# DeltaNet chunks of 128 tokens, an inverse joined from blocks of 32 and 64, and projections given out in two pieces

## The chip, the cores and the metric

The kernel runs on one core of a Trainium2 chip. The metric is device time in microseconds (us) of the whole program: one layer of a hybrid decoder on 1024 tokens of width 1024, in float32. Engines are named as in the profile: PE is TensorE's products and PEld its weight loads, DVE is VectorE, ACT ScalarE, POOL GpSimd, and SP the SyncE queue that issues the DMAs.

## The reference

The layer normalizes x, projects it, runs two token mixers beside each other (a gated DeltaNet and a sparse attention, NSA), merges both by gates, and ends with an MLP. The change touches the DeltaNet alone. Its core, cut to what matters:

```python
DN_HEADS, DN_HEAD_DIM, DN_CHUNK = 8, 128, 64
qkv = silu(causal_depthwise_conv(qkv, conv_w))            # 4 taps
q, k = l2norm(q), l2norm(k);  beta = sigmoid(b_logit)
g = -exp(a_log) * softplus(a_logit + dt_bias)
# per head and chunk of C tokens
gc = cumsum(g);  kb = k * beta;  vb = v * beta
decay = exp(where(causal, gc_i - gc_j, -inf))
a = where(strict, (kb @ k.T) * decay, 0)
u = triangular_solve(a + eye(C), vb)
w = triangular_solve(a + eye(C), kb * exp(gc))
qk = (q @ k.T) * decay;  q_dec = q * exp(gc);  k_end = k * exp(gc_last - gc)
# scan over the chunks, state S (128 x 128)
v_new = u - w @ S
o = q_dec @ S + qk @ v_new
S = S * exp(gc_last) + k_end.T @ v_new
# output: rmsnorm(o) * out_norm * silu(z)
```

The result does not depend on the chunk's length but for rounding: a longer chunk makes fewer steps of the scan and a larger triangular matrix to invert.

## The kernel before, in words

Everything is laid out with features or tokens on the 128 partitions. A projection of the normalized x is a unit of 128 output columns: its weights are read in two DMAs, split on ScalarE and VectorE into a high and a low part (`wh`, `wl`, so that float32 accuracy comes from three fast products), and multiplied with two halves of 512 tokens. One half is 24 products of 128x512, written to a PSUM bank `g` (two banks in turn). A unit of `fill_nb` (the NSA's keys, values and queries) is computed the other way around, in 8 tiles of 128 tokens with 24 products of 128x256 each.

The program is written by a table of due times. `at(step, rank, fn)` enters a function; at the end all are sorted by step and rank and called, and the framework's scheduler then places each engine's instructions. One step is about one half of a projection, 24 streamed products. A head (`head(h, s0)`) covers 24 steps and a new one starts every 14, so the work of two heads overlaps: steps s0 to s0+7 project k, q, v and the gate z with their convolutions; s0+8 to s0+13 are filled with one unit of `fill_nb` and one of `fill_rows` (merge gates); the inverse stands at s0+11 to s0+14, `u_w` at s0+15, and the 16 chunks of 64 tokens from s0+16, three a step, beside the next head's projections.

For a half of 512 tokens (four tiles of 128, two chunks each) `k_natural` and `k_turn` normalize k and make `kbe`, `ke` and the decay matrices `dm`, `qk`; `k_k` and `k_q` multiply k with k and with q. These, the inverse and `u` work on 64 by 64 quadrants of TensorE, the two chunks of a tile on partitions 0 to 63 and 64 to 127. The inverse starts in `blocks`: the diagonal 16 by 16 blocks of all 64 places of a head go through DRAM (`asc`) into a tile of 64 partitions, VectorE eliminates in 15 steps of two small instructions (`xt`, `xi`), and the result comes back through DRAM (`xzs`) as `xa` and its transpose `za`. Then `inv_y` and `inv_x` join blocks of 16 to 32 (level 0) and 32 to 64 (level 1), with a product, an eviction, a product and a subtraction each. `u_w` makes u and w. A `chunk` is a chain: a product with the state (`c<-St,wq`), VectorE's subtraction (`vn`), two products (`c<-vn,ke`, `c<-vn,qk`), VectorE's new state (`St`), and ScalarE's eviction of the output (`o`). Large elementwise products (`kbe`, `ke`, the masks `n1` and `n2`, beta into `dm`, the norm of `o`) run on GpSimd.

After the eighth head come the sparse attention, the merge and the MLP; neither is touched.

Of the kernel before, what the change touches and what calls it, by code (L numbers as in the profile page):

```python
# [30 lines left out]
CH = 64  # L31
# [3 lines left out]
CONST = (("ident", "tri", "blk", "ones", "anyv"), ("m1", "m2", "l1", "l2"),  # L35
# [7 lines left out]
def constants():  # L43
# [4 lines left out]
    same = (p // CH) == (c // CH)  # L48
    ident = (p == c).astype(f)
    tri = (same & (p <= c)).astype(f)  # L50
    blk = same.astype(f)
    i, j = p % CH, np.arange(CH)[None, :]
    m1 = np.where(j < i, 0, 1e30).astype(f)
    m2 = np.where(i <= j, 0, -1e30).astype(f)
    l1 = ((i // 32 == j // 32) & (i // 16 != j // 16)).astype(f)
    l2 = (i // 32 != j // 32).astype(f) + 0 * m1
# [40 lines left out]
    parts = dict(ident=ident, tri=tri, blk=blk, ones=np.ones((128, 128), f), m1=m1, m2=m2, l1=l1, l2=l2, msel=msel,  # L97
# [49 lines left out]
def body(ctx: ExitStack, tc: tile.TileContext, A, out):  # L147
# [146 lines left out]
    def proj(ps, ks, half):  # L294
        sl = slice(half * 512, (half + 1) * 512)
        gemm(ps, [(ks[k][0], ks[k][1], hh[:, k, sl], hl[:, k, sl]) for k in range(8)])
# [100 lines left out]
    def gating():  # L397
# [41 lines left out]
        mm(pg, K("blk"), ln.rearrange("p h t -> p (h t)"), True, True)  # L439
# [143 lines left out]
    def bm(n):  # L583
        return K(n).unsqueeze(1).to_broadcast([128, 4, 64])
# [11 lines left out]
    Q2 = [slice(0, 64), slice(64, 128)]  # L596


    vns = []

    qks = [pd.tile([128, 6, 64], F32, name=f"qk{i}", bufs=1) for i in range(3)]
    for a in qks:
        GP.memset(a, 0.0)
    turn_q = [0]
# [21 lines left out]
    def pairs(l, r):  # L626

        p = PL.ps.tile([128, 4, 64], F32, name="s")
        for i in range(4):
            for q in Q2:  # L630
                mm(p[q, i, :], l[:, i, q], r[:, i, q], True, True)
        return p

# [7 lines left out]

    def move(ap, sl, t, load):

        for q in Q2:
            d = dense(ap, sl)[q, :, q]
            SY.dma_start(t[q] if load else d, d if load else t[q])

    def head(h, s0):
# [11 lines left out]
        def conv(s, half):  # L660

            c0 = 20 + (s * 8 + h) * 4
            ps = gtile()
            proj(ps, H["w", s], half)
# [30 lines left out]
        def k_turn(half):  # L695
# [12 lines left out]
            ut = t4("dm", 2, 64)  # L708
            for q in Q2:
                V.tensor_tensor(ut[q], H["gcB"].rearrange("p (t c) -> p t c", c=128)[q, sl, q],  # L710
                                b3(gc[:, h, sl], 64)[q], OP.subtract)
            H["qk", half] = qks[turn_q[0] % 3]
            turn_q[0] += 1
            dt = H["qk", half][:, 1:5]
# [4 lines left out]
            GP.tensor_tensor(ut, ut, b3(beta[:, h, sl], 64), OP.mult)  # L719
# [12 lines left out]
        def blocks():  # L732
# [17 lines left out]
            for half in range(2):  # L750
                H["x", half], H["z", half] = d = t4("xa", 2, 64), t4("za", 2, 64)
                for j in range(2):
                    move(xz[j], S4[half], d[j], True)

        def row_decay():
            gcB = H["gcB"]
            H["gl"] = gl = pd.tile([128, 16], F32, name="gl", bufs=2)
            act(gl, gcB[:, CH - 1::CH], AF.Exp)
            act(gcB, gcB, AF.Exp)

        def q_sums(half):

# [3 lines left out]
            for i in range(4):  # L766
                for q, o in (Q2, Q2[::-1]):
                    mm(ps[o, i:i + 1], sq[:, i, q], K("ones")[:, 0:1], True, True)
# [5 lines left out]
        def k_q(half):  # L774
            ac = H.pop(("ac", 0, half))
            dt = H["qk", half][:, 1:5]
            V.tensor_tensor(dt, dt, pairs(H["kT", half], ac), OP.mult)
            w = pd.tile([128, 4, 256], F32, name="wq", bufs=2)
            GP.tensor_tensor(w[:, :, 64:192], ac, H["gcB"].rearrange("p (t c) -> p t c", c=128)[:, S4[half]],
                             OP.mult)  # L780
            H["wq", half] = w
# [6 lines left out]

        def gate(half):
            ps = gtile()  # L790
            proj(ps, H["w", 3], half)
# [7 lines left out]
        def inv_y(level, half):  # L799
            H["y", half] = y = t4("y", 2, 64)  # L800
            act(y, each(H["n", half][level], H["z", half]))

        def inv_x(level, half):
            x, z, y = H["x", half], H["z", half], H["y", half]
            p = each(x, y)
            if level == 0:
                p2 = each(y, x)
                V.tensor_tensor(z, z, p, OP.subtract)
                V.tensor_tensor(x, x, p2, OP.subtract)
            else:  # L810
                for q in Q2:
                    V.tensor_tensor(zs[half][q, :, q], z[q], p[q], OP.subtract)

        def u_w(half):
            z, vb = zs[half], H["vb", half]
            u = t2("u", 2)
            p = PL.ps.tile([128, 4, 128], F32, name="s")
            for i in range(4):
                for q in Q2:
                    mm(p[q, i, :], z[q, i, q], vb[q, i, :], True, True)  # L820
            act(u, p)
            H["u", half] = u
            p = four(H["kbe", half], z)
            w = H["wq", half]
            act(w[:, :, 0:64], p[:, :, 0:64])
            act(w[:, :, 192:256], p[:, :, 64:128])

        def chunk(c):
            half, i, q = c // 8, (c % 8) // 2, c % 2
            P_ = slice(64 * q, 64 * q + 64)  # L830
            Q_ = slice(64 - 64 * q, 128 - 64 * q)
            if c % 8 == 0:
                H["o", half] = t2("o", 2)
            o, u, St = H["o", half], H["u", half], H.get("S")
            vn = vns[q]
            ps = PL.pc.tile([128, 128], F32, name="c")
            if St is None:
                V.tensor_copy(vn[P_], u[P_, i, :])
            else:
                mm(ps, H["wq", half][:, i, q * 128:(q + 1) * 128], St, True, False)  # L840
                V.tensor_tensor(vn[P_], u[P_, i, :], ps[P_], OP.subtract)
            if c < 15:
# [7 lines left out]

            k = 64 * (i + q)
            mm(ps, H["qk", half].rearrange("p a b -> p (a b)")[:, k:k + 128], vn, St is None, True)
            act(o[Q_, i, :], ps[Q_], AF.Copy, scale=H["rq", half][Q_, i:i + 1])

        def out_norm(half):
# [6 lines left out]
            GP.tensor_tensor(o, o, b3(ss), OP.mult)  # L862

        def out_turn(half):
            pt = flip(H["o", half], "pc", "c")
            of = t2("of", 1)
            for q in range(2):
                a, b = slice(64 * q, 64 * q + 64), slice(64 - 64 * q, 128 - 64 * q)
                V.scalar_tensor_tensor(of[:, :, a], pt[:, :, b], og, H["sz", half][:, :, a],
                                       op0=OP.mult, op1=OP.mult)  # L870
# [3 lines left out]
        for i, s in enumerate((1, 0, 2, 3)):  # L874
            at(s0 + 2 * i - 2, 2, prep, s)
            for half in range(2):
                if s < 3:
                    at(s0 + 2 * i + half, 1, conv, s, half)
                else:
                    at(s0 + 2 * i + half, 1, gate, half)  # L880
        for half in range(2):
# [6 lines left out]
            at(s0 + 11, 0, inv_y, 0, half)  # L888
# [870 lines left out]
```

## Time and profile before

| what | value |
| --- | --- |
| timed runs, median (lowest to highest) | 2386.36 us (2383.36 to 2388.78) |
| the profiled execution | 2383.02 us, span 2381.2 us |
| busy: PE, PEld | 2330.4 us, 1911.3 us |
| busy: DVE, ACT, POOL | 1600.7 us, 1100.0 us, 292.6 us |
| granted TensorE clock over the span | 0.997 of full |
| one DeltaNet head, first inverse product to the next head's | 112.2 us |

Busy time of PE counts each product to a modelled end, and products overlap, so two of them that start 0.23 us apart are shown with 0.39 us each; the distance of starts is what one costs. A float32 product leaves two records, a transpose one. The streamed products run on a split type and leave one. Idle time is put down to what released the engine; on an engine that is not waited for it costs nothing.

### The profile page before, as it was taken

What the parts mean: (1) busy time and instruction counts of PE and PEld (TensorE: products, weight loads), DVE (VectorE), ACT (ScalarE), POOL (GpSimd) and SP (SyncE); (2) the same over time, 40 slices, a digit from 0 to 9 for tenths busy, and PEclk for the clock granted to TensorE, in tenths of its full rate; (3) what the DMA queues carried; (4) which work ended last, traced back from release to release, by engine and by line L of the source; (5) the groups of instructions that cost most, each with busy time, mean ns of one, the idle gap of its engine ahead of it and who ended that gap; (6) DMA issues with size and microseconds to landing.
All of it is one profiled execution on the core that took longest, in us unless ns stands there. A gap on an engine that the chain in (4) does not pass through costs nothing.

```text
span 2381.2 us, 44200 instructions
## 1 busy us (share of the span) xinstructions
PE 2330.4 (98%) x16657; PEld 1911.3 (80%) x16657; DVE 1600.7 (67%) x3846; ACT 1100.0 (46%) x2274; POOL 292.6 (12%) x299
## 2 busy tenths in 40 slices
PE   7999999999999999999999999999999999999999
PEld 5887878787878797877777778778877888888887
DVE  7666665747574847347868686745498777786875
ACT  4233333424343443226766666542356555544443
POOL 1132321202232333000011111000000000000000
PEclk9999999999999999999999999999999999999999
DMA  6421313131312122227532332055424443495333
GB/s 196 119 62 60 86 43 91 42 94 35 92 46 79 51 70 59 83 83 205 142 110 82 111 94 69 24 179 181 169 102 177 151 155 124 175 325 190 120 115 102
DMA packets 237382, 267.37 MB, mean 112 GB/s; under 512 B 76848, under 2 KB 128368, under 8 KB 237040
## 3 DMA queue, kind: packets, MB, share of 16 engines
q1 hardware_dynamic: 237168, 264.55, 35.3%
q8 instruction: 131, 2.15, 0.4%
q14 instruction: 83, 0.68, 0.1%
HBM read 190.05 MB, written 72.38 MB: 110 GB/s over the span
## 4 chain that ended last, share of the span: by engine, by line
PE 49%; DVE 2%; DMA 1%; ACT 0%; issue 0%; POOL 0%; SPq 0%; ACTq 0%; POOLq 0%; DVEq 0%
PE V L177 20%; PE Q L177 12%; PE T L177 5%; PE o L177 5%; PE g L177 3%; PE S L177 2%; PE m L177 1%; PE m L1280 0%; DVE big L1482 0%; DMA o<-ond 0%; DVE junk L1226 0%; PE m L1193 0%; DMA a<-gtd 0%; POOL acc L1275 0%; DMA ra<-odd 0%
## 5 line engine op out<-in xcount | busy, mean ns | idle before, releaser
L177 PE MATMUL g<-hh,wh 128*128 128x512 f32 (+1 forms) x816 | 336.7, 413 | 7.1 <-ACT hh L174 6.3
L177 PE MATMUL g<-hl,wh 128*128 128x512 f32 (+1 forms) x816 | 328.5, 403 | 0.4 <-DVE hl L327 0.3
L177 PE MATMUL g<-hh,wl 128*128 128x512 f32 (+1 forms) x816 | 325.0, 398 | 0.1
L174 ACT ACTIVATE wh<-a 128x512 fp32r<-128x512 f32 x234 | 146.6, 629 | 248.7 <-PE V L177 155.0
L177 PE MATMUL V<-big,wh 128*128 128x512 f32 x768 | 236.8, 390 | 0.8 <-DVE c L1601 0.8
L1226 DVE CUSTOM_DVE_ANT_0 junk<-S,cst 128x384 f32<-128x384 f32 (+3 forms) x320 | 168.3, 532 | 56.1 <-PE S L177 52.1
L177 PEld LDWEIGHTS g<-hh,wh 128*128 128x128 f32 (+1 forms) x816 | 154.3, 189 | 35.8 <-ACT hh L174 6.8
L174 ACT ACTIVATE P<-T 128x512 f32<-128x512 f32 x228 | 134.2, 597 | 103.4 <-PE T L177 90.5
L186 DVE TENSOR_TENSOR wl<-a,wh 128x512 fp32r<-128x512 f32 x192 | 131.6, 687 | 74.5 <-ACT wh L174 74.4
L177 PEld LDWEIGHTS g<-hh,wl 128*128 128x128 f32 (+1 forms) x816 | 154.2, 189 | 29.3 <-DVE wl L277 0.5
L177 PEld LDWEIGHTS g<-hl,wh 128*128 128x128 f32 (+1 forms) x816 | 154.4, 189 | 28.4 <-DVE hl L327 3.4
L174 ACT ACTIVATE wh<-wr 128x512 fp32r<-128x512 f32 x168 | 105.7, 629 | 153.5 <-PE g L177 127.7
L177 PEld LDWEIGHTS V<-big,wh 128*128 128x128 f32 x768 | 144.1, 188 | 31.5 <-DVE c L1601 1.2
L277 DVE TENSOR_TENSOR wl<-wr,wh 128x512 fp32r<-128x512 f32 x136 | 94.7, 701 | 90.5 <-ACT wh L174 89.5
L177 PE MATMUL V<-big,wl 128*128 128x512 f32 x384 | 149.5, 389 | 0.9 <-DVE wl L277 0.9
L177 PE MATMUL g<-wh,hh 128*128 128x256 f32 x512 | 147.3, 288 | 0.0
L177 PE MATMUL g<-wl,hh 128*128 128x256 f32 x512 | 144.8, 283 | 0.0
L177 PE MATMUL g<-wh,hl 128*128 128x256 f32 x512 | 144.8, 283 | 0.0
L177 PEld LDWEIGHTS o<-vv,P 128*64 128x64 f32 x3648 | 116.0, 138 | 27.1 <-issue 20.4
L177 PE MATMUL o<-vv,P 128*64 128x65 f32 x3648 | 130.1, 225 | 0.0
L177 PE MATMUL S<-ks,qc 96*128 96x384 f32 (+3 forms) x320 | 125.9, 405 | 2.0 <-DVE mx L1226 1.6
L676 DVE SCALAR_TENSOR_TENSOR acc<-xp,cols,acc 128x512 f32<-128x512 f32 x144 | 117.1, 813 | 6.3 <-ACT acc L174 4.8
(381 smaller groups left out, 5462.0 us busy)
## 6 DMA issues: line engine op xcount, KB each, us to landing
bb<-acd SPq DMA_DIRECT2D x112, 256.0 KB, 2.7
wr<-in_w_dn_dram SPq DMA_DIRECT2D x64, 256.0 KB, 2.8
a<-in_w_u_dram SPq DMA_DIRECT2D x64, 256.0 KB, 2.6
acd<-c SPq DMA_DIRECT2D x64, 256.0 KB, 2.2
a<-in_w_d_dram SPq DMA_DIRECT2D x64, 256.0 KB, 3.4
wr<-in_w_nb_dram SPq DMA_DIRECT2D x32, 256.0 KB, 2.7
wr<-in_w_gt_dram SPq DMA_DIRECT2D x32, 256.0 KB, 2.6
gtd<-fx SPq DMA_DIRECT2D x32, 256.0 KB, 2.1
```

Source lines behind the costliest of these rows:

```text
L174: return SC.activation(o, i, fn, **kw)
L177: return PE.matmul(o, l, r, start=start, stop=stop, skip_group_check=True)
L186: V.tensor_tensor(lo, src, f(hi), OP.subtract)
L277: V.tensor_tensor(wl, wr, f(wh), OP.subtract)
L676: V.scalar_tensor_tensor(a2, xp[:, i:i + 512], cols[:, c0 + i:c0 + i + 1], a2, op0=OP.mult, op1=OP.add)
L1226: V.tensor_tensor_reduce(junk[:, :w], ps[:, :w], mask[:, a:b], 1.0, 3e38, OP.add, OP.min, o)
```

## The change

The constant `CH` becomes 128: a tile of 128 tokens is one chunk, so the state goes through 8 steps a head. The decay matrices, masks and products of k with k and with q cover 128 by 128 and use all of TensorE's array. The triangular matrix to invert is 128 wide: one masked level (16 to 32) stays on 64 by 64 quadrants, `join_y` and `join_x` make 64 of 32 with products of 32 columns, and `last_y` and `last_x` make 128 of 64. What GpSimd multiplied is done by four ScalarE instructions each (`rows_by`), or folded into VectorE's instruction on PSUM (`k_k`). A projection's half is given out as `first` (12 products) and, half a step later, the other 12, and `blocks` stands 1.5 steps later. The diff, cut to its core:

```diff
-CH = 64
+CH = 128
...
-    def proj(ps, ks, half):
+    def proj(ps, ks, half, part=(0, 8)):
...
+    def rows_by(o, i, col):
+
+        for j in range(4):
+            act(o[:, j], i[:, j], AF.Copy, scale=col[:, j:j + 1])
...
-            GP.tensor_tensor(kb, kn, b3(beg[:, h, sl]), OP.mult)
+            rows_by(kb, kn, beg[:, h, sl])
...
-            GP.tensor_tensor(k2, kn, b3(ek[:, h, sl]), OP.mult)
+            rows_by(k2, kn, ek[:, h, sl])
...
-            V.tensor_tensor(dm, dm, pairs(H["kT", half], H["kT", half]), OP.mult)
-            move(a_, S4[half], dm, False)
-            n1 = t4("n1", 2, 64)
-            GP.tensor_tensor(n1, dm, bm("l1"), OP.mult)
-            n2 = t4("n2", 2, 64)
-            GP.tensor_tensor(n2, dm, bm("l2"), OP.mult)
-            H["n", half] = (n1, n2)
+            p = four(H["kT", half], H["kT", half])
+            for j in range(4):
+                t = 4 * half + j
+                V.scalar_tensor_tensor(dm[:, j], p[:, j], beta[:, h, t:t + 1], dm[:, j], op0=OP.mult, op1=OP.mult)
+            H["n", half] = n1 = t4("n1", 2, 64)
...
+        def first(s, half):
+            H["g"] = gtile()
+            proj(H["g"], H["w", s], half, (0, 4))
...
+        def join_y(half):
+            dm, z = H["dm", half], zs[half]
+            H["y", half] = y = t4("y", 2, 64)
+            p = PL.ps.tile([128, 4, 64], F32, name="s")
+            for i in range(4):
+                for o in (0, 64):
+                    mm(p[o:o + 32, i, 0:32], dm[o:o + 64, i, o:o + 32], z[o:o + 64, i, o + 32:o + 64], True, True)
+            for o in (0, 64):
+                act(y[o:o + 32, :, 0:32], p[o:o + 32, :, 0:32])
+
+        def join_x(half):
+            x, y, z = H["x", half], H["y", half], zs[half]
+            p = PL.ps.tile([128, 4, 64], F32, name="s")
+            for i in range(4):
+                for o in (0, 64):
+                    mm(p[o:o + 32, i, 0:32], x[o:o + 32, i, 0:32], y[o:o + 32, i, 0:32], True, True)
+                mm(p[32:64, i, 0:32], y[0:32, i, 0:32], x[0:32, i, 0:32], True, True)
+            for o in (0, 64):
+                act(z[o:o + 32, :, o + 32:o + 64], p[o:o + 32, :, 0:32], AF.Copy, scale=-1.0)
+            act(x[32:64, :, 0:32], p[32:64, :, 0:32], AF.Copy, scale=-1.0)
+
+        def last_y(half):
+            a, b = Q2
+            H["y", half] = y = t4("y", 2, 64)
+            p = PL.ps.tile([128, 4, 64], F32, name="s")
+            for i in range(4):
+                mm(p[a, i, :], H["dm", half][b, i, a], zs[half][b, i, b], True, True)
+            act(y[a], p[a])
...
+            act(u, four(zs[half], H["vb", half]))
             H["u", half] = u
...
+            act(H["wq", half][:, :, 0], four(H["kbe", half], zs[half]))
...
+                mm(ps[:, 0], wq[:, i, 0], St, True, True)
+                mm(ps[:, 1], wq[:, i, 1], St, True, False)
+                vn = PL.p2.tile([128, 128], F32, name="vn", bufs=2)
+                V.tensor_tensor(vn, u[:, i], ps[:, 0], OP.subtract)
+            if c < 7:
...
-            at(s0 + 11, 0, inv_y, 0, half)
...
+            at(s0 + 10.5, 0, inv_y, half)
...
-        at(s0 + 5, 0, blocks)
-        for c in range(16):
-            at(s0 + 16 + c // 3, -2, chunk, c)
+        at(s0 + 6.5, 0, blocks)
+        for c in range(8):
+            at(s0 + 16 + c / 2, -2, chunk, c)
```

`last_x` does with `x` and `y` what `last_y` does, and writes the corner of `zs` with the sign turned.

The order of the instructions moves with it. TensorE, a middle head's chunks beside the next head's first projection, before (`St` is the state, `g` a projection's bank, the numbers tell buffers apart):

```order
L177 MATMUL c<-vn_1118,ke 128x128
L177 MATMUL c<-vn_1118,qk_426 128x128
L177 MATMUL g<-hl,wh 128x512
L177 MATMUL g<-hh,wl 128x512
L177 MATMUL c<-St,wq 128x128
L177 MATMUL g<-hh,wh 128x512
L177 MATMUL g<-hl,wh 128x512
L177 MATMUL g<-hh,wl 128x512
L177 MATMUL c<-vn_1116,ke 128x128
```

and the same place after the change:

```order
L174 MATMUL c<-St,wq 128x128 x2
L174 MATMUL g<-hh,wh 128x512
L174 MATMUL g<-hl,wh 128x512
L174 MATMUL g<-hh,wl 128x512
L174 MATMUL g<-hh,wh 128x512
L174 MATMUL g<-hl,wh 128x512
L174 MATMUL g<-hh,wl 128x512
L174 MATMUL c<-vn,ke 128x128
L174 MATMUL c<-vn,qk 128x128
```

Between two links of the chain stand six streamed products where two or three stood, and a link has two products with the state.

TensorE, the second half of a middle head's inverse, before (`za`, `xa` are the inverse and its transpose, `n` the masked matrix, `vb` the values):

```order
L177 MATMUL s<-za,n_4748 64x64 x8
L177 MATMUL s<-za,n_4894 64x64 x8
...
L177 MATMUL s<-y,xa 64x64 x16
...
L177 MATMUL s<-vb,zs_422 64x128 x8
L177 MATMUL s<-zs_422,kbe 128x128 x4
```

and after (`zs` is the joined inverse):

```order
L174 MATMUL s<-zs_422,dm 32x32 x8
L174 MATMUL s<-zs_423,dm 32x32 x8
...
L174 MATMUL s<-y,xa 32x32 x2
L174 MATMUL s<-xa,y 32x32
...
L174 MATMUL s<-zs_422,dm 64x64 x4
L174 MATMUL s<-zs_423,dm 64x64 x4
...
L174 MATMUL s<-y,xa 64x64 x8
...
L174 MATMUL s<-vb,zs_422 128x128 x4
L174 MATMUL s<-zs_422,kbe 128x128 x4
```

One join of two groups has become two joins of two groups each; the pairs of 32 columns stand eight times in a row, for two halves.

VectorE, the start of a middle head's block inverse, before (`ab` is the loaded matrix, `xi` the inverse, `acc` the convolution of v, `vn` and `St` the last chunks of the head ahead):

```order
L744 TENSOR_TENSOR xt<-ab,xi 64x15
L849 SCALAR_TENSOR_TENSOR St<-St,gl,c 128x128
L746 TENSOR_TENSOR xi<-xi,xt 64x15
L676 SCALAR_TENSOR_TENSOR acc<-xp,cols,acc 128x512
L744 TENSOR_TENSOR xt<-ab,xi 64x28
L841 TENSOR_TENSOR vn_1118<-u,c 64x128
L746 TENSOR_TENSOR xi<-xi,xt 64x14x2
```

and after:

```order
L724 TENSOR_TENSOR xt<-ab,xi 64x15
L659 SCALAR_TENSOR_TENSOR acc<-xp,cols,acc 128x512
L726 TENSOR_TENSOR xi<-xi,xt 64x15
L867 TENSOR_REDUCE oss<-of 128x4
L724 TENSOR_TENSOR xt<-ab,xi 64x28
L663 SCALAR_TENSOR_TENSOR acc<-xp,acc 128x512
L726 TENSOR_TENSOR xi<-xi,xt 64x14x2
```

The rows of the chunks are gone from it; the block inverse now begins when the last chunk is done.

## Rows read from the trace of the kernel before

**Rows 1.** The page: span, and each engine's busy us, share, instructions.

```profile
span 2381.2 us, 44200 instructions
PE 2330.4 (98%) x16657; PEld 1911.3 (80%) x16657; DVE 1600.7 (67%) x3846; ACT 1100.0 (46%) x2274; POOL 292.6 (12%) x299
```

**Rows 2.** Stretch of one head: length, busy us by engine (instructions), clock, DMA.

```profile
core 0: us, PE busy (x) PEld busy (x) DVE busy (x) ACT busy (x) POOL busy (x), PEclk, DMA share, GB/s
396.96:509.16 112.20, 109.45 (x861) 92.48 (x860) 66.74 (x160) 39.97 (x78) 22.62 (x20) 1.00 0.23 66
```

**Rows 3.** Timeline of PE, steady projection: start, us, instruction.

```profile
521.18 0.39 PE L177 MATMUL g<-hh,wl 128*128 128x512 f32 x1
...
523.67 0.39 PE L177 MATMUL g<-hl,wh 128*128 128x512 f32 x1
```

**Rows 4.** Timeline of PE at an inverse product among token products.

```profile
508.83 0.28 PE L177 MATMUL g<-wl,hh 128*128 128x256 f32 x1
508.95 0.28 PE L177 MATMUL g<-wh,hl 128*128 128x256 f32 x1
509.16 1.15 PE L177 MATMUL s<-za,n 64*64 64x64 f32 x32
510.24 0.39 PE L177 MATMUL g<-wh,hh 128*128 128x256 f32 x1
510.46 0.28 PE L177 MATMUL g<-wl,hh 128*128 128x256 f32 x1
```

**Rows 5.** Timeline of PE: `u` of a half, then pairs, sums, transposes, chunk.

```profile
537.71 1.09 PE L177 MATMUL s<-vb,zs 64*64 64x128 f32 x16
538.74 1.16 PE L177 MATMUL s<-zs,kbe 128*128 128x128 f32 x8
...
565.24 0.69 PE L177 MATMUL s<-kT 128*64 128x64 f32 x16
565.76 0.58 PE L177 MATMUL tp<-cst,tmp 128*64 128x1 f32 x16
566.27 0.44 PE L609 MATMUL tp<-cst,nat 128*128 128x128 f32 x2
566.55 0.39 PE L177 MATMUL c<-vn,ke 128*128 128x128 f32 x2
566.77 0.39 PE L177 MATMUL c<-vn,qk 128*128 128x128 f32 x2
567.00 0.38 PE L609 MATMUL tp<-cst,nat 128*128 128x128 f32 x2
```

**Rows 6.** Waits of PE, 100 to 1080 us: us in total, times, longest.

```profile
PE c L177 <- DVE vn L841: 8.6, 20, 0.6
PE c L177 <- DVE xi L746: 3.2, 6, 1.2
```

**Rows 7.** Timeline of PE: the last chunk's wait, and one in the chain.

```profile
487.16 0.49 PE L177 MATMUL c<-vn,qk 128*128 128x128 f32 x2 [0.59 <-DVE vn L841]
...
569.99 0.49 PE L177 MATMUL c<-St,wq 128*128 128x128 f32 x2
...
571.59 0.46 PE L177 MATMUL c<-vn,ke 128*128 128x128 f32 x2 [0.41 <-DVE vn L841]
```

**Rows 8.** Timeline of DVE and POOL where both are busy.

```profile
456.59 0.75 DVE L676 SCALAR_TENSOR_TENSOR acc<-xp,cols,acc 128x512 f32<-128x512 f32 x1
457.64 1.39 DVE L676 SCALAR_TENSOR_TENSOR acc<-xp,cols,acc 128x512 f32<-128x512 f32 x1
458.44 1.49 POOL L706 TENSOR_TENSOR ke<-nat,ek 128x512 f32<-128x512 f32 x1
```

**Rows 9.** ScalarE's group of output evictions, 100 to 1080: busy us, mean ns.

```profile
L174 ACT ACTIVATE o<-c,rq 64x128 f32<-64x128 f32 x128 | 46.3, 362 | 130.9 <-PE c L177 120.4 <-DVE acc L676 7.7 <-DVE xp L667 1.9
```

**Rows 10.** Timeline of DVE and SP: one head's block inverse and its DMAs.

```profile
477.51 0.17 DVE L744 TENSOR_TENSOR xt<-ab,xi 64x15 f32<-64x15 f32 x1 [1.63 <-DMA ab<-asc]
493.96 0.37 DVE L747 COPY xi<-xi 64x256 f32<-64x256 f32 x1
493.46 1.47 SPq L749 DMA_DIRECT2D xzs<-xi  x2
496.21 1.26 SPq L646 DMA_DIRECT2D xa<-xzs  x2
500.16 1.27 SPq L646 DMA_DIRECT2D za<-xzs  x2
```

More of the change, by code (lines that the diff above doesn't have):

```diff
@@ L624, in each @@
         return p
[L626 to L632, printed above, removed]
     def diag(ap):
@@ L752, in blocks @@
                 for j in range(2):
-                    move(xz[j], S4[half], d[j], True)
+                    for q in Q2:
+                        SY.dma_start(d[j][q], dense(xz[j], S4[half])[q, :, q])
         def row_decay():
             gcB = H["gcB"]
-            H["gl"] = gl = pd.tile([128, 16], F32, name="gl", bufs=2)
+            H["gl"] = gl = pd.tile([128, 8], F32, name="gl", bufs=2)
             act(gl, gcB[:, CH - 1::CH], AF.Exp)
@@ L766, in q_sums @@
             for i in range(4):
[L767 to L768 removed]
+                mm(ps[:, i:i + 1], sq[:, i, :], K("ones")[:, 0:1], True, True)
             rq = pd.tile([128, 4], F32, name="rq", bufs=4)
@@ L775, in k_q @@
             ac = H.pop(("ac", 0, half))
[L776 to L779, printed above, removed]
+            dt = H["qk", half]
+            V.tensor_tensor(dt, dt, four(H["kT", half], ac), OP.mult)
+            w = pd.tile([128, 4, 2, 128], F32, name="wq", bufs=2)
+            GP.tensor_tensor(w[:, :, 1], ac, H["gcB"].rearrange("p (t c) -> p t c", c=128)[:, S4[half]],
                              OP.mult)
@@ L797, in gate, with inv_y, inv_x @@
             H["sz", half] = s_
-        def inv_y(level, half):
+        def inv_y(half):
             H["y", half] = y = t4("y", 2, 64)
-            act(y, each(H["n", half][level], H["z", half]))
-        def inv_x(level, half):
+            act(y, each(H["n", half], H["z", half]))
+        def inv_x(half):
             x, z, y = H["x", half], H["z", half], H["y", half]
             p = each(x, y)
[L806 to L812, printed above, removed]
+            p2 = each(y, x)
+            for q in Q2:
+                V.tensor_tensor(zs[half][q, :, q], z[q], p[q], OP.subtract)
+            V.tensor_tensor(x, x, p2, OP.subtract)
@@ new lines, in last_y, with last_x @@
+        def last_y(half):
[5 more added lines that the diff above has]
+            act(y[a], p[a])
+        def last_x(half):
+            a, b = Q2
+            p = PL.ps.tile([128, 4, 64], F32, name="s")
+            for i in range(4):
+                mm(p[a, i, :], H["x", half][a, i, :], H["y", half][a, i, :], True, True)
+            act(zs[half][a, :, b], p[a], AF.Copy, scale=-1.0)
@@ L866, in out_turn @@
             of = t2("of", 1)
[L867 to L870, printed above, removed]
+            V.scalar_tensor_tensor(of, pt, og, H["sz", half], op0=OP.mult, op1=OP.mult)
             SY.dma_start(odd[h, :, half * 512:(half + 1) * 512], flat(of))
@@ L876, in head @@
             for half in range(2):
+                at(s0 + 2 * i + half, 1, first, s, half)
                 if s < 3:
-                    at(s0 + 2 * i + half, 1, conv, s, half)
+                    at(s0 + 2 * i + half + 0.5, 1, conv, s, half)
                 else:
-                    at(s0 + 2 * i + half, 1, gate, half)
+                    at(s0 + 2 * i + half + 0.5, 1, gate, half)
         for half in range(2):
@@ L915, in go, with plan @@
             SY.dma_start(dst[:, half * 512:(half + 1) * 512], x)
-        return prep, [lambda s, i=i: at(s, 1, go, i) for i in range(2)]
+        def plan(s, half):
+            at(s, 1, begin, half)
+            at(s + 0.5, 1, go, half)
+        return prep, [lambda s, i=i: plan(s, i) for i in range(2)]
     def fill_nb(u):
@@ L991, in tail_b @@
         pool("p2", side="right")
-        for i in range(2):
-            vns.append(PL.p2.tile([128, 128], F32, name=f"vn{i}", bufs=1))
-            GP.memset(vns[i], 0.0)
     def tail_c():
```

114 lines of the change are left out of this document (47 added, 67 removed).

## The prediction

> **What bounds the kernel now.** I read the page's busy shares first: TensorE is busy for 98% of the span, VectorE for 67%, ScalarE for 46%, GpSimd for 12% [rows 1]. The profiled run took 2383.0 us, 1.8 us more than its span, and 3.4 us less than the median of the three timed runs, 2386.4; I work against 2383.0 and add the 3.4 at the end. Next the stretches: one period of the DeltaNet stage, from one head's first inverse product to the next head's, is 112.2 us at full granted clock, with TensorE marked busy for 109.45 [rows 2]. Eight such periods are the only place where the change acts. So time comes or goes only as TensorE's work in a period, or its waits there, come or go. "Busy" hides part of the waits, because ends of pipelined products are modelled; so I count from one start to the next instead.
>
> **A ledger of one period.** A streamed product of a projection takes 0.2264 us (11 steps from 521.18 to 523.67) [rows 3]; one of the 256-wide token products takes 0.12 us (508.83 to 508.95) [rows 4]. A full float32 product of 128 columns leaves two records of 0.1125 us (four in 0.45 us, 566.55 to 567.00), so 0.225 us; 64-column quadrant products take 0.034 us a record (32 in 1.08 us), 64-column ones over 128 rows 0.0325 (16 in 0.52), one-column sums 0.032 (16 in 0.51), 64-row ones of 128 columns 0.064 (16 in 1.03) [rows 4, 5]. Going from streamed products to small ones and back costs more: 508.95 to 510.46 is 1.51 us, of which one streamed product is 0.12 before, the records 1.08 and one 0.12 after, so about 0.19 us for a round trip [rows 4].
>
> From the code, a period has 240 streamed (54.3 us), 192 token products (23.0), 46 chunk products (15 `St,wq`, 15 `ke`, 16 `qk`: 10.4), 32 transposes (one record each, 3.6), 8 products for `kbe` (1.8), and small ones: 160 records of inverse (5.4), 64 of key and query pairs (2.1), 32 of query sums (1.0), 32 for `u` (2.0), together 10.5. That is 103.6. With 12 round trips, 2.3, it is 105.9, and 6.3 us of the 112.2 are left: waits. The waits I can see belong to the chunk chain. VectorE's `vn` released TensorE 20 times and the rows of the block inverse (`xi`, ahead of `vn` on VectorE) six times [rows 6]; an example is `c<-St,wq` at 569.99, three streamed products, then 0.41 us idle before `c<-vn,ke` at 571.59; the last chunk waits 0.59 us at 487.16 [rows 7].
>
> **The change, part by part, per head.**
>
> *Chunks of 128.* Eight steps instead of sixteen. Seven have two `St,wq` (14), seven a `ke`, eight a `qk`: 29 products against 46. Minus 17 times 0.225 is **-3.8 us**, and this term has no bounds worth the name.
>
> *Pairs, sums and `u` without quadrants.* Key and query pairs become 16 full products, 32 records of 0.1125, 3.6 instead of 2.1. `u` becomes 8 full ones, 1.8 instead of 2.0. The one-column sums become 16 records over 128 stationary columns; the trace has 0.032 for 64 stationary columns and 0.1125 for 128, so 0.5 to 1.8; I take 1.6, near the row with the same stationary size.
>
> *The inverse.* One masked level of 64 by 64 stays: 96 records at 0.034, 3.3. The two last products are 32 records in a single quadrant, where neighbours cannot overlap: between 0.034 (two quadrants in turn) and half of the full 0.1125; I take the upper, 1.8, since that is what 64 columns cost alone. The joins of 32-blocks are 40 products, 80 records of 32 columns, which no row shows. From below the one-column row, 0.032, 2.6; from above half a full record, 4.5; I take 0.034, the nearest small shape, 2.7. The Trainium skill (TensorEngine Tiling (Array Packing), Instruction Overhead) says that a product of few columns costs as much as one of some 60 cycles; by it, an estimate, 25 ns a record, the joins would be 2.0 and the sum 6 us lower over eight heads. No row here goes as low, so I keep the row.
>
> Small work after: 3.6 + 1.8 + 1.6 + 3.3 + 1.8 + 2.7 = 14.8 against 10.5, **+4.3 us** (bounds +2.5 and +6.5). Round trips: pairs, sums and `u` no longer need one; the seven groups of the inverse do, so 7 against 12: **-1.0 us** (0 to -1.5).
>
> *Waits.* In the order of before, three or four streamed products (0.7 to 0.9 us) stand between `c<-St,wq` and `c<-vn,ke`, and two between `ke` and the next `St,wq`; in the new order six and six (1.36 us) at most places. The link needs VectorE's subtraction plus its turn in a queue whose entries take up to 0.75 us, or 1.39 us beside GpSimd [rows 8]. So 1.36 us covers most links; three of seven have fewer products to cover them, and the last head has three streamed ones. The block inverse also moves 1.5 steps later, behind the last chunk, so `xi` no longer stands ahead of `vn`. I give 2.0 us to the seven links and 0.5 us to the handovers of the joins: 2.5 instead of 6.3, **-3.8 us** (bounds 0 and -5.3).
>
> *What costs nothing.* GpSimd's products of `kbe`, `ke` and the output go to ScalarE, four instructions each. At 0.362 us, the row of `o<-c,rq` that has this width [rows 9], 24 more of them a head are 8.7 us, on an engine with 40 us busy in 112 [rows 2]; that leaves ScalarE under half, and `kbe` and `ke` are read only a dozen steps later, by `u_w` and the chunks. What the bursts may delay instead is in rival 2. Masks of 512 columns instead of 256 on VectorE are balanced by half as many `St` and `vn`. Giving a projection out in two pieces moves no product; it only lets a chunk stand every half step. A constant table is 128 columns shorter at the start: under half a microsecond.
>
> *A wait that could grow.* The block inverse is a chain by way of DRAM: its first VectorE row starts at 477.51 and its copy at 493.96, 16.4 us, of which about 30 tiny rows are 6 us and the rest other work; two stores follow at 493.46, eight loads until 501.43, and the first inverse product waits until 509.16, so some 5 us of slack after a landing of about 2 us, the time from first store to first load being 2.75 [rows 4, 10]. Moved 1.5 steps later (8.2 us), with the product half a step earlier (2.9 us), the slack would be -6 us; but nine `St` and `vn` and the masks of the next head leave its VectorE stretch, by the order about 4 us of work, and its load is issued at the head of the gate step instead of a projection's tail (2.5 us). I make it near +1 us: no wait, but no cover.
>
> *Sum.* -3.8 + 4.3 - 1.0 - 3.8 = -4.3 us a head. The first head fills and the last drains differently (three streamed products only); I take 7.5 heads, -32 us: 2351 for the profiled run, **2354 us** against the median, 1.3% faster.
>
> **Rivals.**
> 1. *The waits stay.* If VectorE and ScalarE answer as late as now, the chain keeps its 6.3 us: -0.5 us a head, 2382, about no change. For it: the last chunk waited though nine streamed products stood before it [rows 7], so distance alone does not cure a late queue. Against it: that VectorE stretch held the block inverse, which moves. 13%.
> 2. *The inverse becomes the wait (slower).* Place: the first inverse product of each head, and the five handovers PE, ScalarE, PE behind it at one half-step (2.7 us) each. If the block inverse takes as long as now after its first row, its loads land 3 to 4 us after the product's turn, and five handovers at 0.7 us, one row of ScalarE queue, add 3.5: 7 us a head, 8 heads, +56 on 2354, 2410. It decides from 4.3 us of new waits a head. A burst of eight ScalarE rows (2.9 us) ahead of an `o` that frees the chunk's bank would act in the same way. Against it: VectorE and ScalarE are idle for 45 and 72 us of the 112 [rows 2]. 11%.
> 3. *More comes back.* With GpSimd's large products gone, VectorE's 1.39 us instruction beside `ke` (1.49 us on GpSimd) is 0.75 us again, and no chunk waits: 2.5 us a head more, and cheap joins, 1 us: 7.5 times 3.5 is 26 more, 2328. The Trainium skill (SBUF — State Buffer, "SBUF: two separate sides") says that GpSimd and a VectorE instruction with two SBUF inputs exclude each other for a whole instruction; the 1.39 beside 0.75 [rows 8] agrees, and by the rule this rival gains most. Against it: VectorE is not the bound, so what it gains reaches the end only where TensorE waited. 14%.
>
> **How the numbers follow.** My forecast, -32 give or take 16 us (2338 to 2372), has 62%. Its terms at their favourable bounds give -8 us a head, 2322; at the unfavourable ones +2.7, 2407. From these and the rivals the range for 8 in 10 is 2328 to 2384. About 0.2%, 5 us, is what a measurement of this kernel can tell from no change: the forecast, rival 3 and a quarter of rival 1 make faster 0.81; the rest of rival 1 and a little of rival 2 make the same 0.10; slower 0.09.
>
> **What would show it.** Right: a period near 108 us; `St,wq`, `ke` and `qk` records near 29 products a head at 0.11 us; joins near 0.03 us a record; no idle row over 0.3 us before `c<-vn,ke` in the middle heads; GpSimd busy under 200 us. Wrong: joins near 0.06 us, idle time before `s<-za,n` released by a load of `xa` or `za`, or before `s<-zs,dm` and `s<-vb,zs` released by ScalarE; or a period still near 112 us, with the waits on `vn` as long as now.

## The result, and the profile after

The changed kernel took 2354.89 us, median of four runs (2353.76 to 2355.44), against 2385.77 us of the kernel before in the same session: a ratio of 0.9869, 95% interval [0.9852, 0.9886], or 27 to 35 us less. The forecast was 2354. The number came out; the step on the waits behind it did not, nor did all that was put at nothing, and two parts of the change turned out to work against each other.

The page of the profiled execution, in answer to [rows 1]; it took 2355.1 us:

```profile
span 2353.3 us, 43197 instructions
PE 2306.0 (98%) x16257; PEld 1917.6 (81%) x16257; DVE 1567.3 (67%) x3742; ACT 1155.6 (49%) x2482; POOL 184.2 (8%) x198
```

TensorE is busy for 24 us less, GpSimd for 108 us less, ScalarE for 56 us more. One head, in answer to [rows 2] (length, busy time by engine, granted clock):

```profile
495.96:606.07 110.11, 107.10 (x816) 93.63 (x815) 65.44 (x158) 48.75 (x110) 12.91 (x12) 1.00 0.24 67
```

From first inverse product to first inverse product, the first six periods were 113.0 us on average before (170.79 to 848.60) and are 109.9 now (166.96 to 826.55): 3.0 us a head, where 4.3 were forecast. These six periods whole, before and after (length, busy time of TensorE and of the others):

```profile
170.79:848.60 677.81, 664.44 (x5225) 561.99 (x5224) 428.07 (x1056) 261.58 (x533) 170.50 (x152) 1.00 0.23 66
```

```profile
166.96:826.55 659.59, 645.53 (x4925) 565.51 (x4924) 401.91 (x979) 303.01 (x689) 89.91 (x80) 1.00 0.24 67
```

TensorE's idle time, length less busy time, was 13.4 us and is 14.1 us: 2.2 and 2.3 us a head. The gain is all in its products. Giving each of TensorE's rows the time up to the next row's start, less the idle time that the timeline shows between them, splits a head's period so (us, mean of the six, each figure rounded for itself):

| | before | after | difference |
| --- | --- | --- | --- |
| the chunks' products | 10.1 | 6.2 | -3.9 |
| small work: pairs, sums, `u`, inverse | 11.0 | 14.1 | +3.1 |
| transposes and the products for `kbe` | 6.5 | 6.1 | -0.3 |
| streamed and token products, the same 432 | 83.2 | 81.2 | -2.0 |
| idle | 2.2 | 2.3 | +0.1 |
| period | 113.0 | 109.9 | -3.0 |

The waits of TensorE on the chunks, 100 to 1050 us, in answer to [rows 6] (waiting line, what released it: us in total, times, longest):

```profile
PE c L174 <- DVE vn L850: 9.2, 13, 0.8
PE c L174 <- DVE xp L652: 4.4, 6, 0.8
PE s L174 <- DMA za<-xzs: 1.4, 3, 0.7
```

The first two are 13.6 us in 19 waits, not less than the 8.6 and 3.2 us of before (11.8 in 26). (`xp` in the second line is a memset that ended when `vn` did; `vn` is what was waited for.) They stand at the same three places in each of the middle heads. The first two look alike; here is one, on TensorE, GpSimd and VectorE (start, us, line, out<-in; the idle time before it in brackets):

```profile
442.26 0.61 PE L174 MATMUL c<-St,wq 128*128 128x128 f32 x4
...
443.40 0.40 PE L174 MATMUL g<-hh,wh 128*128 128x512 f32 x1
444.53 0.46 PE L174 MATMUL c<-vn,ke 128*128 128x128 f32 x2 [0.73 <-DVE vn L850]
```

```profile
442.46 1.01 POOL L239 TENSOR_TENSOR ss<-ss,mhalf 128x4 f32<-128x4 f32 x1 [7.86 <-DVE ss L238]
```

```profile
442.22 0.16 DVE L238 TENSOR_SCALAR ss<-ss 128x4 f32<-128x4 f32 x1
443.50 0.69 DVE L675 TENSOR_TENSOR nat<-tp,ss 128x512 f32<-128x512 f32 x1 [1.12 <-POOL ss L239]
444.11 0.28 DVE L850 TENSOR_TENSOR vn<-u,c 128x128 f32<-128x128 f32 x1
```

The product with the state is done at 442.9, but `vn` stands in VectorE's queue behind `nat`, and `nat` waits for GpSimd's power of 128 by 4 numbers, which takes a microsecond. The third place has another cause: VectorE's row for `qk` takes 1.72 us beside GpSimd's product for `wq`, which the change left on GpSimd, and only four `kT` products (eight records, 1.06 us) cover the link; TensorE then idles for 0.78 us.

```profile
445.16 1.30 POOL L758 TENSOR_TENSOR wq<-acc,gcB 128x512 f32<-128x512 f32 x1 [1.69 <-PE c L174]
```

```profile
445.29 1.72 DVE L694 TENSOR_TENSOR qk<-dm,cst 128x512 f32<-128x512 f32 x1
...
448.73 0.27 DVE L850 TENSOR_TENSOR vn<-u,c 128x128 f32<-128x128 f32 x1
```

The new small products, first record and what follows it (answers to [rows 4, 5]):

```profile
512.17 0.39 PE L174 MATMUL g<-hh,wl 128*128 128x512 f32 x1
512.49 0.69 PE L174 MATMUL s<-zs,dm 64*32 64x32 f32 x32
513.12 0.50 PE L174 MATMUL g<-hh,wh 128*128 128x512 f32 x1
513.46 0.39 PE L174 MATMUL g<-hl,wh 128*128 128x512 f32 x1
...
518.79 0.22 PE L174 MATMUL s<-y,xa 32*32 32x32 f32 x2
...
519.29 0.19 PE L174 MATMUL s<-xa,y 32*32 32x32 f32 x1
...
522.36 1.14 PE L174 MATMUL s<-zs,dm 64*64 64x64 f32 x16
523.43 0.50 PE L174 MATMUL g<-hh,wh 128*128 128x512 f32 x1
```

```profile
449.68 0.95 PE L174 MATMUL tp<-cst,tmp 128*128 128x1 f32 x8
450.49 0.63 PE L606 MATMUL tp<-cst,nat 128*128 128x128 f32 x4
```

Joins, from the first record to the next streamed product: 32 records in 0.63 us, and 48 in 0.63 (518.79 to 519.42), so 0.020 and 0.013 us a record. The last level: 16 records in 1.07 us, 0.067 each. The sums: 8 in 0.81, 0.10 each.

### The profile page after: what moved, and what is told of

The parts are those of the page before. It is cut to its first block, busy times and chain, and to the rows that moved or that the text cites. A ratio compares the mean times of both kernels' runs of the same rounds, so it can differ in the third digit from the quotient of the medians.

```text
span 2353.3 us, 43197 instructions
## 1 busy us (share of the span) xinstructions
PE 2306.0 (98%) x16257; PEld 1917.6 (81%) x16257; DVE 1567.3 (67%) x3742; ACT 1155.6 (49%) x2482; POOL 184.2 (8%) x198
## 4 chain that ended last, share of the span: by engine, by line
PE 86%; DVE 6%; DMA 2%; issue 2%; ACT 1%; POOL 1%; SPq 0%; ACTq 0%; POOLq 0%; DVEq 0%
PE g L174 31%; PE V L174 20%; PE Q L174 12%; PE T L174 5%; PE s L174 5%; PE o L174 5%; PE S L174 2%; PE c L174 2%; PE m L174 1%; POOL ss L239 1%; PE tp L606 1%; DVE wl L274 1%; PE tp L174 1%; DVE junk L1238 0%; DVE acc L659 0%
## 5 line engine op out<-in xcount | busy, mean ns | idle before, releaser
L174 PE MATMUL g<-hl,wh 128*128 128x512 f32 (+1 forms) x816 | 322.8, 396 | 0.1
L174 PE MATMUL Q<-big,wh 128*128 128x512 f32 x384 | 118.4, 390 | 0.7 <-ACT wh L171 0.5
```

The source lines that it names most:

```text
L174: return PE.matmul(o, l, r, start=start, stop=stop, skip_group_check=True)
```

## The experiments

Each kernel is the changed one or the one before with one edit, timed in three rounds (the joins in one) beside the kernel before. Where two kernels differ by less than some 4 us I read the DeltaNet stage alone: the same first inverse product came at 165.5 to 170.8 us in different kernels' profiles. The kernel before itself took 2385.8, 2384.5, 2384.5 and 2383.3 us in the four sessions, the result's and the three of the experiments, so a difference of 2 us between kernels of two sessions shows nothing.

**GpSimd's products back.**

```diff
-            rows_by(kb, kn, beg[:, h, sl])
+            GP.tensor_tensor(kb, kn, b3(beg[:, h, sl]), OP.mult)
-            rows_by(k2, kn, ek[:, h, sl])
+            GP.tensor_tensor(k2, kn, b3(ek[:, h, sl]), OP.mult)
-            rows_by(o, o, ss)
+            GP.tensor_tensor(o, o, b3(ss), OP.mult)
```

> The changed kernel with its three large GpSimd products (kbe, ke, the norm of o) given back to GpSimd; everything else as changed. My theory (TensorE's products and the waits before c<-vn,ke make the time; GpSimd's part is hidden): 2350 to 2362, at most one vn a head later by the 0.6 us that a VectorE product loses beside GpSimd (8 x 0.6 = 5 us). Rival (the freed VectorE port is where the gain comes from): most of the 31 us is lost again, 2370 or more.

2378.76 us, ratio 0.9978 [0.9969, 0.9987]: 24 us of the 31 are gone, and my theory with them. What happened shows at the third place. GpSimd, VectorE and TensorE there:

```profile
564.24 1.49 POOL L689 TENSOR_TENSOR ke<-nat,ek 128x512 f32<-128x512 f32 x1
565.69 1.72 POOL L758 TENSOR_TENSOR wq<-acc,gcB 128x512 f32<-128x512 f32 x1
```

```profile
565.01 1.27 DVE L694 TENSOR_TENSOR qk<-dm,cst 128x512 f32<-128x512 f32 x1
566.20 1.76 DVE L274 TENSOR_TENSOR wl<-wr,wh 128x512 fp32r<-128x512 f32 x1
...
569.09 0.27 DVE L850 TENSOR_TENSOR vn<-u,c 128x128 f32<-128x128 f32 x1
```

```profile
566.31 1.06 PE L174 MATMUL s<-kT 128*128 128x128 f32 x8
569.51 0.46 PE L174 MATMUL c<-vn,ke 128*128 128x128 f32 x2 [2.14 <-DVE xp L652]
...
572.37 0.63 PE L174 MATMUL g<-hl,wh 128*128 128x512 f32 x1
572.79 0.63 PE L174 MATMUL g<-hh,wl 128*128 128x512 f32 x1
```

`ke` pushes `wq` back, to 0.68 us after the start of `qk` instead of 0.13 us before it, so that both of VectorE's rows ahead of `vn` are slow, 1.27 and 1.76 us, and TensorE stands still for 2.14 us. After that its clock falls: streamed products start 0.42 us apart where they take 0.226, and the stretch behind the wait has a granted clock of 0.66, a mix of its two levels (2.4 and 1.2 GHz):

```profile
565.00:570.00 5.00, 2.86 (x21) 2.53 (x20) 4.97 (x8) 3.75 (x7) 2.42 (x2) 1.00 0.20 46
570.00:575.00 5.00, 5.00 (x24) 4.35 (x23) 4.81 (x12) 2.23 (x4) 1.01 (x1) 0.66 0.08 19
```

It fell to 0.55 to 0.68 in the 5 us behind five of the six such waits. In the first six periods TensorE's idle time is 22.1 us (676.93 less 654.86) instead of 14.1, and its busy time 654.9 instead of 645.5 for the same 4925 records: 8.0 us of waits and 9.3 us of slower products. That is the 17.3 us by which these periods grew; all seven grew by 18 (799.3 against 781.1). The profile is of the run of 2374.66 us; over the ten runs the granted clock of the whole span goes from 0.993 down to 0.988 and the time up to 2384.53, so a typical run loses some 4 us more than the profile shows.

**Projections whole.** Both pieces of a half at the same step, also in the fills:

```diff
-                    at(s0 + 2 * i + half + 0.5, 1, conv, s, half)
+                    at(s0 + 2 * i + half, 1, conv, s, half)
...
-            at(s + 0.5, 1, go, half)
+            at(s, 1, go, half)
...
-                at(s + t % 2 / 2, 1, go, t)
+                at(s, 1, go, t)
...
-                    at(s + 2 + t % 2 / 2, -0.5, turn, t)
+                    at(s + 2, -0.5 + 0.1 * (t % 2), turn, t)
```

> The changed kernel with each half projection given out whole again, so that two chunks of 128 stand between two halves; the order then has 2 to 3 streamed products where six stood at three of the links, and 15 or 16 at the others. My theory (cover of a link counts): these links wait 0.5 to 1 us each, 1.5 to 3 us a head, 2367 to 2379. Rival (the chain of 8 is short enough, the split brings nothing): 2355 give or take 3.

2352.01 us, ratio 0.9864 [0.9849, 0.9878]: no slower than in pieces. Fewer streamed products stand in three of the links, and yet the waits on `vn` are nearly gone (compare 9.2 and 4.4):

```profile
PE c L174 <- DVE vn L850: 1.3, 2, 0.7
```

In the heads from 390 to 604 us `vn` starts 0.3 to 0.95 us after the last record of its product with the state begins; in the changed kernel, at its three late links, it is 1.5 to 2.0 us. So neither distance nor the chain's length made the waits; what stands ahead of `vn` in VectorE's queue did. `nat` still waits for GpSimd, 1.07 us at 443.58, but the product with the state comes only after it, at 444.67.

**Both back.** The last two edits together.

> The changed kernel with projections given out whole and the three products (kbe, ke, norm of o) on GpSimd: both parts undone at once. Theory (GpSimd's products cost 24 us only because the pieces put a chunk's vn into VectorE's queue just behind rows that GpSimd slows or holds): with the other order they cost little, 2351 to 2362. Rival (they cost 24 us in any order of chunks of 128): 2372 to 2380.

2351.31 us, ratio 0.9860 [0.9842, 0.9877]. With the other order GpSimd's products cost nothing that can be measured. They are as long as ever, but lie where no `vn` waits; VectorE's `vn` beside them in one head:

```profile
550.07 1.35 POOL L686 TENSOR_TENSOR kbe<-nat,beg 128x512 f32<-128x512 f32 x1 [0.87 <-DVE nat L675]
551.38 1.76 POOL L758 TENSOR_TENSOR wq<-acc,gcB 128x512 f32<-128x512 f32 x1
553.09 1.49 POOL L689 TENSOR_TENSOR ke<-nat,ek 128x512 f32<-128x512 f32 x1
```

```profile
551.12 0.28 DVE L850 TENSOR_TENSOR vn<-u,c 128x128 f32<-128x128 f32 x1
...
555.98 0.28 DVE L850 TENSOR_TENSOR vn<-u,c 128x128 f32<-128x128 f32 x1
```

The four corners, chunks of 128 throughout:

| | in pieces | whole |
| --- | --- | --- |
| products on GpSimd | 2378.8 | 2351.3 |
| products on ScalarE | 2354.9 | 2352.0 |

The 24 and 27 us between the corner at 2378.8 and its two neighbours are clear of the noise; the 3 and the 1 us between the others are not.

**`ke` alone on GpSimd**, the second pair of lines of the first diff.

> The changed kernel with ke alone given back to GpSimd, kbe and the norm of o left on ScalarE. Theory (ke and then wq on GpSimd make VectorE's qk and wl rows slow ahead of one vn a head, TensorE waits 2.2 us and its clock falls after it): most of the 24 us is there, 2370 to 2380, with one wait of about 2 us a head. Rival (the three products add up, or the norm of o does it): 2355 to 2363.

2366.45 us, ratio 0.9929 [0.9912, 0.9945]: 11.6 us, half of the 24, so neither side was right. `qk` and `wl` are slow here too (1.36 and 1.78 us), but the wait is 1.5 us instead of 2.1, and in the profiled run, of 2362.74 us, the clock fell (0.66) after one of the six; the three other runs took 2365.45 to 2367.73 us at a clock of 0.994 to 0.995 over the span, where the profiled one has 0.997:

```profile
PE c L174 <- DVE xp L652: 9.0, 6, 1.5
```

**The kernel before with the three products on ScalarE**, by `rows_by`, chunks still of 64.

> The kernel before with only its three GpSimd products (kbe, ke, the norm of o) done by four ScalarE instructions each, chunks still of 64. My theory now (a product on GpSimd costs where a chunk's vn stands in VectorE's queue just then, and the long waits that stop TensorE come with chunks of 128): the two waits of 0.5 us a head behind VectorE's 1.2 to 1.4 us rows go, 8 us: 2374 to 2382. Rival (GpSimd's products cost 24 us by themselves, whatever the chunk): 2357 to 2364, and then the longer chunk brings only the rest.

2386.09 us, ratio 1.0003 [0.9993, 1.0012]: nothing, against both. The two waits a head stayed (10.1 us on `vn` in 25 times): each `vn` stands behind a tap of the convolution all the same. At 456.45 such a tap still takes 1.40 us, beside `wq` (455.89 to 457.30), which this edit left on GpSimd. So the run does not tell what all of GpSimd's products cost with chunks of 64.

**The kernel before in pieces**, chunks of 64 at `s0 + 16 + c / 3`. One chunk of a head, due at `s0 + 18.33`, then reads a decay matrix that the next head's `k_turn`, due at `s0 + 18`, has already written; this adds a dependence, so that the total isn't the price of the pieces alone.

> The kernel before with projections given out in two pieces and its 16 chunks at every third of a step (s0 + 16 + c / 3 where c // 3 stood), chunks still of 64. My first theory (distance covers a link) would have the excess before St,wq and vn of about 3.8 us a head go to 2 or less: 2365 to 2375. Rival (the order decides little, as giving projections out whole again cost nothing in the changed kernel): 2384 give or take 5.

2401.40 us, ratio 1.0071 [1.0056, 1.0086]: slower, against both. The waits on `vn` are three times those of before, and the longest shows the same pattern as the changed kernel, here behind `rq`, another row that waits for GpSimd's power, to which GpSimd came only after its two mask products:

```profile
PE c L177 <- DVE vn L848: 26.1, 22, 1.7
```

```profile
590.01 0.17 DVE L774 TENSOR_SCALAR rq<-rq 128x4 f32<-128x4 f32 x1 [1.59 <-POOL rq L242]
590.09 0.27 DVE L848 TENSOR_TENSOR vn<-u,c 64x128 f32<-64x128 f32 x1
```

The profiled run took 2404.11 us. Of its excess 12.5 us lie in the seven periods (817.7 against 805.2), and TensorE's waits for ScalarE's `dm`, 5.8 us in five times, which the kernel before does not have, are likely the added dependence. Another 9.7 us lie behind the last head's first inverse product, where the granted clock was 0.91 from 1050 to 1150 us (0.98 before); why is open.

**`nat` later.** The changed kernel, `nat` taken out of `k_natural` into `k_scale`.

```diff
-            V.tensor_tensor(kn, ps, b3(ss), OP.mult)
...
+            at(s0 + 2.5 + half, -1.9, k_scale, half)
```

> The changed kernel with VectorE's nat<-tp,ss, which waits for GpSimd's power, called half a step later than the sums; by the order it moves behind one vn<-u,c a head of the two that it stood ahead of. My theory (vn waits in VectorE's queue behind nat): one of the three waits of 0.84 to 0.94 us before c<-vn,ke goes and two stay, 8 x 0.9 = 7 us, 2346 to 2350. Rival (the chain is late for another reason, such as the product with the state itself): 2355 give or take 3, three waits a head as before.

2356.40 us, ratio 0.9879 [0.9863, 0.9895]. The wait went as foreseen (6.1 us in 7 times, from 9.2 in 13), and the seven periods are 776.4 us instead of 781.1; the total doesn't show it. This profile's clock is 0.994 over the span (0.997 in the changed kernel's); what follows the last head's first inverse product took 3.8 us more. I can't say that this will be so in each run.

**`nat` on ScalarE.**

```diff
-            V.tensor_tensor(kn, ps, b3(ss), OP.mult)
+            rows_by(kn, ps, ss)
```

> The changed kernel with nat done by four ScalarE instructions from PSUM, so that VectorE's queue never waits for GpSimd's power there. My theory: the two waits behind nat go (8 x 1.75 = 14 us), less what the six more ScalarE rows of 0.39 us and ScalarE's own wait for GpSimd (about 1 us) delay: 2341 to 2350. Rival (ScalarE's queue is as tight: o and the weights' splits now wait for GpSimd instead): 2353 to 2370.

2353.52 us, ratio 0.9871 [0.9856, 0.9885]: the same as the change. The two waits behind `nat` are smaller or gone, but `vn` now meets `rq`, and the sum on `vn` is 9.6 us again:

```profile
564.43 0.17 DVE L750 TENSOR_SCALAR rq<-rq 128x4 f32<-128x4 f32 x1 [0.90 <-POOL rq L239]
564.51 0.28 DVE L850 TENSOR_TENSOR vn<-u,c 128x128 f32<-128x128 f32 x1
```

**`wq` on VectorE.**

```diff
-            GP.tensor_tensor(w[:, :, 1], ac, H["gcB"]
+            V.tensor_tensor(w[:, :, 1], ac, H["gcB"]
```

> The changed kernel with the product for wq (q times its decay) on VectorE instead of GpSimd, so that VectorE's qk row of 1.72 us ahead of the third late vn of a head should be 0.7. Theory (that row makes the third wait of 0.94 us): the wait before c<-vn,ke behind the kT products goes from 0.8 to about 0, 5 to 7 us, 2347 to 2351; the two waits behind nat stay. Rival (VectorE's own new row of 0.7 us takes the place): 2353 to 2358.

2355.81 us, ratio 0.9882 [0.9865, 0.9899]. The third wait went (the 4.4 us put down to `xp` are 0) and `qk` takes 0.69 us, so the wait's cause is shown; the time did not follow. Part came back as waits for the inverse's loads, 2.6 us instead of 1.4; the periods are only 2.6 us shorter in all.

**Each `ke` product twice.**

```diff
                 mm(p2, H["ke", half][:, i, :], vn, True, True)
+                mm(p2, H["ke", half][:, i, :], vn, True, True)
```

> The changed kernel with each chunk's product with ke issued twice, 7 more a head. Theory (a chunk's product stands on the path with its full 0.225 us, which the -3.8 us of the prediction rests on): 56 x 0.225 = 12.6 us, 2366 to 2370. Rival (the chunk's products lie in waits that are there anyway): 2355 to 2361. Rival (the state, and with it the next link, comes later and waits more): 2373 or more.

2377.58 us, ratio 0.9972 [0.9961, 0.9983]: 22.7 us more, the last of the three. The seven periods grew by 19.1 us. In the first six TensorE's busy time grew by 9.6 us (655.11 against 645.53) for 84 more records, 0.114 each, and its idle time by 5.2. The waits on `vn` grew from 13.6 to 21.1 us (25 times, the longest 2.2). So a chunk's product costs its full time, and the longer link more on top.

**No joins.** `join_y`, `join_x`, `last_y` and `last_x` not called.

> The changed kernel without join_y, join_x, last_y and last_x (the corners of the inverse stay out): 112 records and four handovers a head less. By the prices of the prediction (1.8 + 2.7 + 4 x 0.19 us a head) it would be 42 us faster, 2313; by the starts in the changed kernel's trace (2.2 + 1.3 + 0.8) 34 us, 2321. Rival (the inverse's handovers make a wait as well): 45 us or more, 2310 or less. Rival (the inverse is hidden in waits that stay): 2340 or more.

2341.73 us, ratio 0.9823 [0.9804, 0.9843]: 13 us instead of 34. Three of the first six periods fell by the 4 us that the rows say (106.0 against 109.9); in the others the loads of the inverse are late, and one of these has a granted clock of 0.97:

```profile
PE s L174 <- DMA za<-xzs: 8.1, 14, 1.2
```

**The inverse half a step earlier**, on top of whole projections.

```diff
-            at(s0 + 10.5, 0, inv_y, half)
+            at(s0 + 10, 0, inv_y, half)
...
-        at(s0 + 6.5, 0, blocks)
+        at(s0 + 6, 0, blocks)
```

> The changed kernel with projections given out whole, and the block inverse and the first four steps of the inverse half a step earlier, so that a whole half projection stands between every two steps of the inverse. Theory (with whole projections the waits left are the handovers of the inverse, 0.6 to 1.7 us a head): 2342 to 2350. Rival (the loads of za and xa, which have no slack, become the wait, as they did where the joins were left out): 2352 to 2362.

2363.00 us, ratio 0.9919 [0.9895, 0.9943]: the rival, 11 us slower than whole projections alone; in the profiles 8 us of it lie in the seven periods (783.8 against 775.8). The handovers no longer wait, the loads do:

```profile
PE s L174 <- DMA za<-xzs: 8.4, 15, 1.0
```

So no version stands clear of the change: whole projections are 3 us faster (2349.7 to 2354.1 against 2353.8 to 2355.4), in a session in which the kernel before was 1 us faster too, and the intervals of the two ratios overlap.

## Why the prediction was right, and where it was not

**The chunks' products (-3.8 us): right.** They came to -3.9 a head, and `ke_twice` shows that they lie on the path.

**Small work (+4.3): right in sign, 1.1 too high.** By the rows of after: pairs 3.6, `u` 1.8, sums 1.6, masked level 3.3, last products 2.1, joins 1.3; 13.7 against 10.5 is +3.2, and counted over the six periods it is +3.1. The joins were costed at 0.034 us a record and took 0.020 and 0.013. The prediction's estimate of 25 ns, worked out from the Trainium skill (TensorEngine Tiling (Array Packing), Instruction Overhead), is above these rows as well. The one-quadrant products cost 0.067, not half of 0.1125.

**Round trips (-1.0): right in price, wrong in number.** 508.95 to 510.46 in [rows 4] gave 0.19 us a trip; 512.17 to 513.46 after is 1.29 us with two streamed products (0.45) and the 0.63 of the records, so 0.2 us again. But the 12 and 7 trips left out the chunks. In the timelines the run of streamed and token products is broken 36.7 times a head before and 26.7 times after, and 28 and 14 of these breaks begin with a row of the chunks' bank `c`. Ten breaks fewer at 0.2 us are the -2.0 us of the table.

**Waits (-3.8): the step that failed.** "6.3 us of the 112.2 are left: waits" took all that the ledger did not explain for waits. Only 2.2 us a head were idle time. The rest was mainly the breaks that were not counted (83.2 us for products that would take 77.4 at 0.2264 and 0.12 us each, so 5.8 us where 2.3 were counted), and the transposes of `nx`, 1.3 us a head, that the ledger lacks. Of the idle time nothing went: 2.2 became 2.3. "So 1.36 us covers most links" took the subtraction's own time and one queue entry, and my mark for it, no idle row over 0.3 us before `c<-vn,ke`, failed at three rows in every middle head. What decides is whether a row that waits for GpSimd, or runs beside it, is ahead of `vn` at that moment. With whole projections and GpSimd's products put back, the same products come in a period of 108.84 us, and the idle time is 1.0 us a head:

```profile
169.22:822.24 653.02, 647.05 (x4926) 563.71 (x4925) 419.24 (x979) 265.42 (x544) 131.50 (x116) 1.00 0.24 68
```

**"What costs nothing": half wrong.** Giving a projection out in two pieces moves no product, as I wrote, but it moves `vn` behind `nat` and the slow rows: 27 us with the products on GpSimd, and nothing clear of the noise with them on ScalarE. And GpSimd's products are not hidden: taking them off is worth 24 us in this order and nothing in the other. Rival 3 was right that VectorE's rows are slow beside GpSimd, 1.27 to 1.78 us against 0.68 to 0.75, and wrong that the change would end this, since `wq` stayed there. The 1.39 us of [rows 8] stood beside `wq` too, and the kernel before without `ke` on GpSimd still shows 1.40. The rule quoted there (the Trainium skill, SBUF — State Buffer, "SBUF: two separate sides") agrees: `qk`, begun 0.13 us after `wq`, ended 0.55 us after it.

**The inverse without cover: right.** "Near +1 us: no wait, but no cover": 1.4 us of waits in all in the changed kernel, 0 to 2.7 in the other kernels with chunks of 128, but over 8 us in the two that leave the joins out or call the inverse half a step earlier. Rival 2 had the place right.

**The sum.** 3.0 instead of 4.3 us in six periods, 18 us; the first inverse product came 3.8 us earlier, the last interval is 6.0 shorter and the rest 0.1 longer: 28 us of span against the 32 forecast. The wait term was 3.9 us a head too good; the round trips, the small work and the transposes together gave back 2.5. That these misses cancel for the most part, and that the ends gave 9.7 where I had counted a head and a half (6.5), is why the number is so near; it is luck, not working. What carries the gain is the chunk of 128 with its joined inverse (and the masks, the beta and the later places in the order that moved with it, not tried apart): alone it gives 2351.3 us, 32 less than the kernel before in its session. The other two parts only undo each other.

Three small sums of the prediction are off: the terms at their favourable bounds give 2326 us (the 3.4 us were not added), -32 give or take 16 is 2338 to 2370, and the shares named for faster add up to 0.79. None of them moves the forecast.

## What to carry to other kernels

Before you call the rest of a ledger waits, compare it with the idle time of the profile: here most of it was the price of switching between streamed and small products. A queue whose next instruction waits for a tiny operation on another engine holds up whatever is behind it, as `nat` held `vn`; look at what stands ahead of the critical instruction there, not only at how much work covers it on the engine that waits. Parts of a change that seem hidden can be worth tens of microseconds together and nothing apart: undo them in a square of four, not one by one. When the main chain becomes shorter, ask which slack it has eaten: here the inverse's loads became the wait in two of the kernels tried.

## What the runs showed of the hardware

GpSimd's power of 128 by 4 numbers takes 1.0 to 1.3 us on average, longer than VectorE's 128 by 512 product (0.69), and VectorE was idle for 15.3 us ahead of 16 `nat` rows because of it:

```profile
L239 POOL TENSOR_TENSOR ss<-ss,mhalf 128x4 f32<-128x4 f32 x16 | 20.4, 1274 | 349.7 <-DVE ss L238 349.7
```

```profile
L675 DVE TENSOR_TENSOR nat<-tp,ss 128x512 f32<-128x512 f32 x16 | 11.1, 692 | 15.3 <-POOL ss L239 15.3
```

And stops of TensorE within full work are not all alike. Behind those of 2.1 us (GpSimd's products back) the granted clock fell below 0.7 over the next 5 us in five cases of six, behind those of 1.5 us (`ke` alone) in one of six, and behind those of 1.7 us in the kernel before in pieces in none of six, each in one profiled run. It also fell, to 0.67, behind the one stop of 2.2 us with each `ke` product twice, and to 0.66 behind one of 1.2 us without the joins. Length alone doesn't settle it; what does was not tried.
